# Delta rule of a three-layer trunk: modulation loads of four row tiles, one transpose for a group, multiplies from GpSimd to VectorE, substitution beside the recurrence

## The chip, the core and the metric

The program runs on one core of one Trainium2 chip. The metric is the device time of one execution in microseconds (us). Three executions of the kernel before took 2703.0, 2703.69 and 2696.82 us; the median is 2703.0 us.

The core's engines are named as the profile names them: PE is TensorE's matmul stream and PEld its loads of weights, DVE is VectorE, ACT is ScalarE, POOL is GpSimd, SP is the queue that issues most of the loads. Each engine runs its own list of instructions in order; a scheduler at build time writes these lists from the program, with semaphores between engines.

## The reference

A hybrid block (window attention beside a gated delta rule, both gated and merged, then an MLP), followed by two more layers. All is fp32, 512 latent tokens and 256 context tokens of width 1024. The change lies in the delta rule of the first block and in what is run beside it. Cut to that:

```python
# 8 heads of 64, chunks of 64 tokens, two directions; 6 tiles of 128 tokens = 12 chunks a direction
kk     = einsum('bhnid,bhnjd->bhnij', kc, kc)
t_mat  = eye(64) + bc[..., :, None] * dec_strict * kk
w_mat  = triangular_solve(t_mat, (bc * eG)[..., None] * kc)      # unit lower triangular
u_v    = triangular_solve(t_mat, bc[..., None] * vc)
intra  = dec_incl * einsum('bhnid,bhnjd->bhnij', qc, kc)
q_dec  = eG[..., None] * qc
k_tail = exp(g_last[..., None] - G)[..., None] * kc
def step(S, xs):                                                   # lax.scan over the 12 chunks
    u = uv_c - w_c @ S
    o = qd_c @ S + intra_c @ u
    S = exp(gl_c) * S + k_tail_c.T @ u
    return S, o
# beside it, independent of it: modulations silu(c) @ w_ada + b_ada of both conditioning vectors,
# and the attention half of the merge: sigmoid(gate_a) * (y_a @ w_br_attn)
```

## The kernel before

The work around the change is `delta`, a method that block 1 calls after its projections. It treats six token tiles (order 0, 1, 2, 5, 3, 4), in three groups of two steps of both directions; a group holds 64 triangular systems of 64 (chunk, step, direction, head). Its parts are Python generators:

- `prep(t)` makes a tile's matrices: `M` (decay times k k^T times the write strength b), and for latent tiles `R` (the masked intra-chunk matrix) and `qd` (q times its decay). The multiplies by b (L936), by the mask (L944) and of qd (L946) are on POOL.
- `subst(g)` inverts the 32 x 32 diagonal blocks of a group by substitution. Four DVE transposes of 32 partitions each (L957) make `Lw` from `M`; then come 31 steps of a DVE multiply into `tmp` (L964) and a DVE subtract into `X` (L966).
- `merges(g)` makes the inverses of the 64 x 64 systems from `X`: eight DVE transposes of 32 partitions (L981, L982) into two arrays `O1` and `O2`, products of 32 x 32 (L990, L1000, L1003) with a copy `Pm` on ACT between them (L994), and copies into place on ACT (L1006) and DVE (L1007).
- `chain(g, d)` is the recurrence of one direction over a group's two tiles. It loads k and v and scales them on POOL (L1021), makes `WT` (L1034, copied on ACT at L1036) and the first part of `u` (L1043). Per chunk it adds WT times the state to `u` (L1055), copies `u` on ACT (L1057), scales the old state into `Sg` on POOL (L1061), multiplies k and u into `d` (L1068) and sets the new state S = Sg + d on DVE (L1077; L1075 for the first). Per latent tile it then makes the output: for each half of 64 partitions four products of qd and S (L1084), then eight of R and u (L1087).
- `output` norms, gates and transposes the finished tiles of the last group (L1104 to L1121), after which the first dense product of the merge can start (L449 on `yDh`).

Two generators of other work run beside the recurrence. `attn_half` makes the attention half of the merge (PE products L449 on `yAh` and `yAl`, the split of the weights into `whi` on ACT and `wlo` on POOL at L731, the gate's multiply on DVE at L740). `ada` makes modulations: a load of one row tile (128 rows) by 512 columns, 256 KB, on the SP queue (L194), then one fp32 matmul of 32 output columns by 512 (L203) into one of four 32-partition groups of a PSUM bank; there are 96 such loads. `behind` holds each step of this other work behind the last but one product of the recurrence.

The order of the parts comes from `weave` and `side_by_side`, which take steps of several generators in proportion to given numbers of steps, and from the scheduler. Before: all preps with `subst(0)` between them, beside dense products; then `merges(0)`, `subst(1)` and `subst(2)` beside the rest of the dense products; then the recurrence of groups 0, 1 and 2 with `merges(1)` beside group 0 and `merges(2)` beside group 1:

```python
self.weave((seq(merges(0, *N, op), subst(1), subst(2)), 72), (early[0], early[1] - 20))
...
self.weave((seq(self.side_by_side((both(0), 28), (mg[1], 8)), self.side_by_side((both(1), 28), (mg[2], 8)),
                both(2)), 105), *[(self.behind(x, marks), n) for x, n in late(ch)])
```

## Time and profile before

| what | value |
|---|---|
| median of three executions | 2703.0 us |
| span of the profiled execution, first to last instruction | 2700.1 us |
| PE busy | 2514.3 us, 93% |
| PEld busy | 2108.0 us, 78% |
| DVE busy | 1498.9 us, 56% |
| ACT busy | 976.2 us, 36% |
| POOL busy | 992.4 us, 37% |
| mean granted TensorE clock | 0.961 |

The profile was taken on one execution; its time as a run is not given beside its span, so the span is what sums are made against, and the median lies 2.9 us above it. Busy shares are means over stages with different limits. The stage of the change lies between about 398 us and 712 us of the span: at 398 us DVE is in `subst(0)` and the preps, at 469 us `merges(0)` starts, at 512 us the first state is set, at 696 us the last `u` is done, and at 711.7 us the first dense product on the recurrence's result starts.

### The profile page before, as it was taken

What the parts mean: (1) busy time and instruction counts of PE and PEld (TensorE: products, weight loads), DVE (VectorE), ACT (ScalarE), POOL (GpSimd) and SP (SyncE); (2) the same over time, 40 slices, a digit from 0 to 9 for tenths busy, and PEclk for the clock granted to TensorE, in tenths of its full rate; (3) what the DMA queues carried; (4) which work ended last, traced back from release to release, by engine and by line L of the source; (5) the groups of instructions that cost most, each with busy time, mean ns of one, the idle gap of its engine ahead of it and who ended that gap; (6) DMA issues with size and microseconds to landing.
All of it is one profiled execution on the core that took longest, in us unless ns stands there. A gap on an engine that the chain in (4) does not pass through costs nothing.

```text
span 2700.1 us, 39906 instructions
## 1 busy us (share of the span) xinstructions
PE 2514.3 (93%) x15890; PEld 2108.0 (78%) x15890; DVE 1498.9 (56%) x2449; ACT 976.2 (36%) x1788; POOL 992.4 (37%) x829
## 2 busy tenths in 40 slices
PE   5897997799889999999999999999999999999998
PEld 3786875456677778889887888888888887888888
DVE  4556559993458972252585695757225447522225
ACT  3545443122342322342474522222223356423332
POOL 2443214534453323355334522333234623523331
PEclk8998998799899999999999999999999999999999
DMA  7231264455724643221012153434212101322231
GB/s 257 73 96 47 77 163 146 133 182 161 242 82 158 186 154 99 95 73 48 9 37 93 59 156 113 153 98 145 63 63 63 62 13 47 102 94 94 94 107 50
DMA packets 237625, 282.53 MB, mean 105 GB/s; under 512 B 12935, under 2 KB 183550, under 8 KB 237182
## 3 DMA queue, kind: packets, MB, share of 16 engines
q1 hardware_dynamic: 214062, 249.87, 29.6%
q10 hardware_dynamic: 23376, 30.11, 3.4%
q8 instruction: 125, 2.05, 0.3%
q14 instruction: 62, 0.51, 0.1%
HBM read 264.06 MB, written 15.88 MB: 104 GB/s over the span
## 4 chain that ended last, share of the span: by engine, by line
PE 72%; DVE 16%; DMA 4%; issue 4%; ACT 3%; POOL 1%; SPq 0%; ACTq 0%; POOLq 0%; DVEq 0%
PE mm L449 58%; DVE aacc L244 3%; DMA wada<-in_w_ada_dram 3%; PE mm L203 2%; PE sc L1796 2%; PE mm L1821 1%; DVE nt L315 1%; DVE wlo L108 1%; DVE X L966 1%; DVE tmp L964 1%; PE u L1055 1%; PE mm L1830 1%; PE mm L1327 1%; DMA wst<-in_w_in_dram 1%; PE mm L1084 1%
## 5 line engine op out<-in xcount | busy, mean ns | idle before, releaser
L108 POOL TENSOR_TENSOR wlo<-wst,whi 128x1024 fp32r<-128x1024 f32 (+2 forms) x143 | 374.3, 2619 | 812.4 <-ACT whi L437 798.5
L437 ACT ACTIVATE whi<-wst 128x1024 fp32r<-128x1024 f32 (+2 forms) x293 | 288.1, 1031 | 662.1 <-PE mm L449 365.6
L449 PE MATMUL mm<-hmxl,whi 128*128 128x512 f32 (+1 forms) x816 | 314.6, 387 | 5.0 <-DVE hmxl L318 2.7
L449 PE MATMUL mm<-hmxh,whi 128*128 128x512 f32 (+1 forms) x816 | 310.7, 386 | 7.3 <-ACT hmxh L317 7.3
L449 PE MATMUL mm<-hmxh,wlo 128*128 128x512 f32 (+1 forms) x816 | 312.6, 385 | 2.8 <-DVE wlo L108 2.8
L449 PE MATMUL mm<-hidxl,whi 128*128 128x512 f32 (+1 forms) x720 | 280.7, 390 | 7.7 <-DVE hidxl L1451 7.5
L449 PE MATMUL mm<-hidxh,wlo 128*128 128x512 f32 (+1 forms) x720 | 280.1, 389 | 1.1 <-DVE wlo L108 1.1
L108 DVE TENSOR_TENSOR wlo<-wst,whi 128x1024 fp32r<-128x1024 f32 (+1 forms) x150 | 184.4, 1232 | 170.8 <-ACT whi L437 170.7
L449 PE MATMUL mm<-hidxh,whi 128*128 128x512 f32 (+1 forms) x720 | 277.3, 388 | 0.0
L244 DVE SCALAR_TENSOR_TENSOR aacc<-wada,silu,aacc 128x512 f32<-128x512 f32 x280 | 244.7, 922 | 27.4 <-DMA wada<-in_w_ada_dram 27.0
L331 DVE SCALAR_TENSOR_TENSOR xres<-mm,mod,xres 128x512 f32<-128x512 f32 (+1 forms) x122 | 85.1, 703 | 236.0 <-PE mm L449 235.8
L1447 POOL TENSOR_TENSOR nsq<-nt 128x512 f32<-128x512 f32 (+1 forms) x134 | 135.5, 1014 | 151.6 <-ACT nt L1446 128.7
L449 PEld LDWEIGHTS mm<-hmxl,whi 128*128 128x128 f32 x816 | 158.2, 194 | 36.2 <-DVE hmxl L318 4.0
L449 PEld LDWEIGHTS mm<-hmxh,whi 128*128 128x128 f32 x816 | 156.6, 194 | 37.9 <-ACT hmxh L317 8.3
L449 PEld LDWEIGHTS mm<-hmxh,wlo 128*128 128x128 f32 x816 | 157.9, 194 | 33.8 <-DVE wlo L108 4.0
L1451 DVE TENSOR_TENSOR hidxl<-nsq,hidxh 128x512 fp32r<-128x512 f32 (+1 forms) x102 | 74.7, 732 | 168.2 <-POOL nsq L1447 165.7
L449 PEld LDWEIGHTS mm<-hidxl,whi 128*128 128x128 f32 x720 | 136.1, 189 | 38.3 <-DVE hidxl L1451 10.5
L449 PEld LDWEIGHTS mm<-hidxh,wlo 128*128 128x128 f32 x720 | 136.2, 189 | 30.2 <-DVE wlo L108 2.0
L449 PEld LDWEIGHTS mm<-hidxh,whi 128*128 128x128 f32 x720 | 136.2, 189 | 28.1
L1446 ACT ACTIVATE nt<-mm 128x512 f32<-128x512 f32 (+1 forms) x134 | 69.6, 521 | 231.6 <-PE mm L449 228.7
L449 PE MATMUL mm<-hh,whi 128*128 128x512 f32 x256 | 106.0, 414 | 7.5 <-DVE cy L625 3.3
L449 PE MATMUL mm<-whi,h2xh 128*128 128x256 f32 x384 | 110.1, 289 | 3.0 <-ACT raw L1579 2.6
(521 smaller groups left out, 6204.0 us busy)
## 6 DMA issues: line engine op xcount, KB each, us to landing
wst<-in_w_mlp_dram SPq DMA_DIRECT2D x96, 1024.0 KB, 5.4
wada<-in_w_ada_dram SPq DMA_DIRECT2D x256, 256.0 KB, 3.0
wst<-in_w_in_dram SPq DMA_DIRECT2D x35, 1024.0 KB, 5.5
wst<-in_w_out_dram SPq DMA_DIRECT2D x10, 1024.0 KB, 7.4
wada<-in_w_ada_dram SPq DMA_DIRECT2D x8, 1024.0 KB, 14.3
xacc<-in_w_out_dram SPq DMA_DIRECT2D x16, 256.0 KB, 2.9
Gb<-grows SPq DMA_DIRECT2D x12, 256.0 KB, 4.9
kc<-tok_k ACTq DMA_DIRECT2D x12, 256.0 KB, 3.6
```

The costliest lines, as they stand in the source:

```text
L108: e.tensor_tensor(out, x, hi.bitcast(F32), ALU.subtract)
L203: nc.tensor.matmul(ps[32 * g:32 * g + 32, :], sT[:, k, 30 - 2 * i:62 - 2 * i], loaded[x][:, k - k0, :], start=i == 0 and k < 4, stop=i == ...
L244: nc.vector.scalar_tensor_tensor(acc[j], wt, c, acc[j], ALU.mult, ALU.add)
L315: nc.vector.scalar_tensor_tensor(t, x[:, k, :], a(k), self.rb[n], ALU.mult, ALU.mult)
L331: nc.vector.scalar_tensor_tensor(x[:, m, :], ps[:, :T], gate(m, n), x[:, m, :], ALU.mult, ALU.add)
L437: self.nc.scalar.activation(hi[:, :, c0:c1], st[:, :, c0:c1], AF.Copy)
L449: self.nc.tensor.matmul(ps, lhs[a](k), rhs[b](k), start=first and i == 0, stop=last and i == n - 1)
L964: nc.vector.tensor_tensor(t, Lw[:, j + 1:, j:j + 1].to_broadcast([P, n, w]), x[:, j:j + 1, 0:w].to_broadcast([P, n, w]), ALU.mult)
L1446: nc.scalar.activation(t, ps[:, :T], AF.Relu)
L1447: nc.gpsimd.tensor_tensor(s2, t, t, ALU.mult)
L1451: self.latest = nc.vector.tensor_tensor(lo, s2, hi.bitcast(F32), ALU.subtract)
L1796: mm = nc.tensor.matmul(ps[:, c0:c1], QT_[:, w, t * P:(t + 1) * P], KT_[:, c0:c1], start=w == 0, stop=w == 1)
```

## The change

It leaves the arithmetic of the result as it is and alters how and where it is done:

1. `ada` loads four row tiles by 256 columns (512 KB) instead of one row tile by 512 (256 KB): 48 loads instead of 96, each followed by four matmuls of 32 x 256 into the four partition groups, one behind the other.
2. `subst`: ACT copies the four diagonal blocks of `M` into the other X buffer, and one DVE transpose of 128 partitions makes `Lw`.
3. `merges`: two DVE transposes of 128 partitions, into `Z2` and `Z1`, instead of eight of 32; the products read `Z1` and `Z2`, and eight ACT copies place their blocks into `O`. There is one `O` for a group (instead of two), in `M[0]` and `M[1]` for the later groups.
4. Multiplies go from POOL to DVE: M by b, R by the mask, qd (now straight from the PSUM tile of the transposes), the scaling of k and v, Sg, `wlo` of `attn_half`, and the gate z of `output`.
5. The output of a latent tile makes the R products first, alternating between the two halves of the partitions, then those of qd and S.
6. `merges(0)` alone stands beside the rest of the dense products; `subst(1)` and `merges(1)` run beside the recurrence of group 0, `subst(2)` and `merges(2)` beside that of group 1. The given numbers of steps are 160 (105 before) and 50 for the modulations (25 before).

Comments and docstrings go too, so line numbers shift by a few: L203 becomes L201, L449 L447, L957 L960 (with the ACT copies at L959), L964 and L966 become L967 and L969, L981 and L982 L984 and L985 (with the ACT copies at L1011), L994 L997, L1021 L1029, L1061 L1069, L1077 L1085, L1084 L1096, L1087 L1092.

```diff
-    def ada(self, pool, sT, w, bias, mod, n0, n1, kc=4, depth=1, bufs=None):
+    def ada(self, pool, sT, w, bias, mod, n0, n1, W=512, depth=1, bufs=None):
...
-        parts = [(i, k) for i in range(nb) for k in range(0, KT, kc)]
+        parts = [(i, k, c) for i in range(nb) for k in range(0, KT, 4) for c in range(0, 512, W)]
...
-                nc.tensor.matmul(ps[32 * g:32 * g + 32, :], sT[:, k, 30 - 2 * i:62 - 2 * i], loaded[x][:, k - k0, :],
-                                 start=i == 0 and k < 4, stop=i == nb - 1 and k >= 4)
+            for g in range(4):
+                nc.tensor.matmul(ps[32 * g:32 * g + 32, c:c + W], sT[:, k0 + g, 30 - 2 * i:62 - 2 * i],
+                                 loaded[x][:, g, :], start=i == 0 and k0 == 0 and c == 0,
+                                 stop=i == nb - 1 and k0 > 0 and c + W == 512)
...
-                        nc.gpsimd.tensor_tensor(lo, st, hi.bitcast(F32), ALU.subtract)
+                        nc.vector.tensor_tensor(lo, st, hi.bitcast(F32), ALU.subtract)
...
+                if src is qt:
+                    qd4 = qd.rearrange("p (d r) t -> p d r t", d=2)
+                    nc.vector.tensor_tensor(qd4, qd4, pt.rearrange("p (r t) -> p r t", t=P).unsqueeze(1)
+                                            .to_broadcast([P, 2, 4, P]), ALU.mult)
...
-                nc.gpsimd.tensor_tensor(m, m, b, ALU.mult)
+                nc.vector.tensor_tensor(m, m, b, ALU.mult)
...
+            Md = self.T(one, [P, 32, 32], f"X{1 - g % 2}")
             for b in range(4):
                 sl, cs = slice(32 * b, 32 * b + 32), slice(32 * (b % 2), 32 * (b % 2) + 32)
-                nc.vector.transpose(Lw[sl], M[g][sl, :, cs].rearrange("a p r -> a r p"))
+                nc.scalar.activation(Md[sl], M[g][sl, :, cs], AF.Copy)
+            nc.vector.transpose(Lw, Md.rearrange("a p r -> a r p"))
...
-            for b in range(4):
-                sl, cs = slice(32 * b, 32 * b + 32), (lo, hi)[b % 2]
-                nc.vector.transpose(O1[sl, :, cs].rearrange("a p r -> a r p"), x[sl])
-                nc.vector.transpose(O2[sl, :, cs].rearrange("a p c -> a c p"), x[sl].rearrange("a r c -> a c r"))
-                yield
+            Z1, Z2 = (self.T(pool, [P, 32, 32], n, bufs=1) for n in ("Z1", "Z2"))
+            nc.vector.transpose(Z2.rearrange("a p c -> a c p"), x.rearrange("a r c -> a c r"))
+            nc.vector.transpose(Z1.rearrange("a p r -> a r p"), x)
+            yield
...
+                if q0 == 0:
+                    for b in range(4):
+                        sl, cs = slice(32 * b, 32 * b + 32), (lo, hi)[b % 2]
+                        for d, z in enumerate((Z1, Z2)):
+                            nc.scalar.activation(parts(O[sl], d)[:, :, :, cs], parts(z[sl], d), AF.Copy)
...
-                    nc.gpsimd.tensor_tensor(x, y, dl[f][:, t, d, :].unsqueeze(2).to_broadcast([P, 8, CH]), ALU.mult)
+                    nc.vector.tensor_tensor(x, y, dl[f][:, t, d, :].unsqueeze(2).to_broadcast([P, 8, CH]), ALU.mult)
...
-                            nc.gpsimd.tensor_tensor(
+                            nc.vector.tensor_tensor(
                                 Sg[e], S0[e, :, e], dl["egs"][e, c, d, t, :].unsqueeze(2).to_broadcast([CH, 4, CH]),
                                 ALU.mult)
...
+                    for h in range(8):
+                        for c in half:
+                            nc.tensor.matmul(ps[c, h * CH:(h + 1) * CH], R[c, d, h, :], u[c, h, :],
+                                             start=h == 0, stop=False)
                     for c, S0 in states:
                         for r in range(4):
                             nc.tensor.matmul(ps[half[c], r * P:(r + 1) * P], qd[:, d, r, half[c]], S0[:, r, :],
-                                             start=r == 0, stop=False)
-                        for h in range(8):
-                            nc.tensor.matmul(ps[half[c], h * CH:(h + 1) * CH], R[half[c], d, h, :], u[half[c], h, :],
-                                             start=False, stop=h == 7)
+                                             start=False, stop=r == 3)
...
-        self.weave((seq(merges(0, *N, op), subst(1), subst(2)), 72), (early[0], early[1] - 20))
+        O = [self.T(op, [P, 32, CH], "O0"), M[0], M[1]]
+        self.weave((merges(0, O[0], op), 5), (early[0], early[1] - 20))
...
-        self.weave((seq(self.side_by_side((both(0), 28), (mg[1], 8)), self.side_by_side((both(1), 28), (mg[2], 8)),
-                        both(2)), 105), *[(self.behind(x, marks), n) for x, n in late(ch)])
+        nxt = lambda g: (seq(subst(g), merges(g, O[g], op)), 37)
+        self.weave((seq(self.side_by_side((both(0), 28), nxt(1)), self.side_by_side((both(1), 28), nxt(2)),
+                        both(2)), 160), *[(self.behind(x, marks), n) for x, n in late(ch)])
```

On PE, in the recurrence of group 1, the kernel before has these rows: modulation products (L203, out of a `wada` tile) stand singly or in twos and fours between products of the recurrence.

```order
L1055 MATMUL u_6117<-S_715_4527,WT_946_6042 64x128 x4
L203 MATMUL mm_953_6090<-wada_6180,silu_90_410 32x512
L203 MATMUL mm_953_6090<-wada_6183,silu_90_410 32x512
L1084 MATMUL mm_987_6261<-S_715_4527,qd_3919 64x128 x2
L203 MATMUL mm_953_6090<-wada_6186,silu_90_410 32x512
L1084 MATMUL mm_987_6261<-S_715_4527,qd_3919 64x128 x2
L1087 MATMUL mm_988_6290<-u_970_6144,R_3999 64x64
L203 MATMUL mm_953_6090<-wada_6227,silu_90_410 32x512
```

After, at the same kind of place (the start of group 1, beside the products of its `merges`), the modulation products (L201) come in fours, half as wide, from one `wada` tile.

```order
L201 MATMUL mm_725_4440<-wada_4995,silu_93_423 32x256 x4
L993 MATMUL mm_829_5166<-Z_821_5044,M_595_3399 32x32 x32
L201 MATMUL mm_725_4440<-wada_5022,silu_93_423 32x256 x4
L201 MATMUL mm_725_4440<-wada_5092,silu_93_423 32x256 x4
L1051 MATMUL u_5334<-vc_789_4834,M_594_3398 64x64
L1051 MATMUL u_5370<-vc_795_4868,M_594_3398 64x64
L201 MATMUL mm_725_4440<-wada_5160,silu_93_423 32x256 x4
```

The four of one load have moved together. On ACT, where `merges(0)` makes the first group's inverses, the kernel before goes from the loads and the weight split straight to the copies `Pm`.

```order
L1018 DMA kc_753_4671<-tok_k_448 128x512
L1019 DMA vc_754_4672<-tok_v_449 128x512
L994 ACTIVATE Pm_4134<-mm_687_4101 32x512 x2
L1006 ACTIVATE O_685_4079<-mm_689_4137 32x8x32
L994 ACTIVATE Pm_4207<-mm_690_4174 32x512 x2
```

After, the eight copies into `O` (L1011) and the four of the next group's diagonal blocks (L959, `X` out of `M`) stand ahead of the first `Pm` (L997).

```order
L1026 DMA kc_751_4552<-tok_k_448 128x512
L1027 DMA vc_752_4553<-tok_v_449 128x512
L1011 ACTIVATE O_686_4081<-Z_688_4095 32x2x8x32 x4
L1011 ACTIVATE O_686_4081<-Z_687_4094 32x2x8x32 x4
L959 ACTIVATE X_718_4403<-M_595_3399 32x1024 x4
L997 ACTIVATE Pm_4167<-mm_694_4134 32x512 x2
```

Twelve copies have come ahead of what the second product of `merges(0)` reads. On DVE, at the end of `subst(1)`, the kernel before has the last step, four transposes for the next group, eight for this one, and then the next group's steps.

```order
L966 TENSOR_TENSOR X_699_4268<-X_699_4268,tmp_4269 128x31
L957 STREAM_TRANSPOSE Lw_4382<-M_596_3400 32x1024 x4
L981 STREAM_TRANSPOSE O_712_4524<-X_699_4268 32x32x32
L982 STREAM_TRANSPOSE M_594_3398<-X_699_4268 32x32x32
...
L964 TENSOR_TENSOR tmp_4384<-Lw_4382,X_704_4383 128x31
L740 TENSOR_TENSOR ga_4773<-mm_803_4965,ga_4773 128x512
L1077 TENSOR_TENSOR S_715_4527<-Sg_813_5017,d_5071 64x4x64 x2
```

After, two transposes stand there, and behind them states (L1085), scalings of k (L1029) and of states (L1069), which POOL had before.

```order
L969 TENSOR_TENSOR X_716_4401<-X_716_4401,tmp_4402 128x31
L729 TENSOR_TENSOR wlo_4650<-wst_4645,whi_4649 128x512
L738 TENSOR_TENSOR ga_4534<-mm_768_4674,ga_4534 128x512
L984 STREAM_TRANSPOSE Z_821_5044<-X_716_4401 128x32x32
L985 STREAM_TRANSPOSE Z_820_5043<-X_716_4401 128x32x32
L1085 TENSOR_TENSOR S_709_4388<-Sg_766_4661,d_4699 64x4x64 x2
L1085 TENSOR_TENSOR S_712_4391<-Sg_769_4688,d_4718 64x4x64 x2
L1029 TENSOR_TENSOR kb_790_4835<-kc_788_4833,gnb_947 128x512
L1069 TENSOR_TENSOR Sg_803_4909<-S_709_4388,gegs_895 64x256 x2
L1069 TENSOR_TENSOR Sg_805_4927<-S_712_4391,gegs_895 64x256 x2
```

Nine transposes fewer stand around that place (the one into `Lw` comes nine rows further on), and the multiplies of the recurrence have come into DVE's list. From the end of `delta` on, the engines' lists are the same in both kernels but for a few exchanged neighbours.

## Rows read from the trace of the kernel before

**Rows 1.** Windows (start:end length, busy us and instructions by engine, clock, DMA share, GB/s):

```profile
core 0: us, PE busy (x) PEld busy (x) DVE busy (x) ACT busy (x) POOL busy (x), PEclk, DMA share, GB/s
398.00:469.00 71.00, 51.95 (x445) 40.90 (x443) 66.60 (x103) 23.60 (x31) 32.12 (x20) 0.89 0.49 149
469.00:512.00 43.00, 27.14 (x462) 17.19 (x462) 41.26 (x59) 7.61 (x16) 25.85 (x34) 0.62 0.36 115
512.00:696.00 184.00, 177.06 (x2254) 109.27 (x2254) 111.76 (x177) 41.79 (x82) 65.46 (x75) 0.97 0.57 179
696.00:712.00 16.00, 8.55 (x54) 5.22 (x54) 8.38 (x16) 3.54 (x7) 3.24 (x2) 0.71 0.54 191
```

**Rows 2.** Chain that ended last, 469 to 712: first piece, first PE piece of eight (start, us):

```profile
468.13 1.93 DVE O L981
...
518.34 3.64 PE mm L449 x8
```

**Rows 3.** Window of L203 alone (PE and PEld busy), 512 to 696:

```profile
512.00:696.00 184.00, 57.78 (x162) 8.06 (x162) 0.97 0.57 179
```

**Rows 4.** PE timeline, modulation products (start, us, two or eight records):

```profile
522.52 1.05 PE L203 MATMUL mm<-wada,silu 128*32 128x512 f32 x2
...
618.40 1.06 PE L203 MATMUL mm<-wada,silu 128*32 128x512 f32 x8
```

**Rows 5.** Window of L1087 alone (PE and PEld busy), 512 to 696:

```profile
512.00:696.00 184.00, 17.52 (x234) 15.10 (x234) 0.97 0.57 179
```

**Rows 6.** PE timeline, products of 64 x 64, halves not alternating and alternating:

```profile
653.34 1.09 PE L1087 MATMUL mm<-u,R 64*64 64x64 f32 x16
...
669.79 1.14 PE L1043 MATMUL u<-vc,O 64*64 64x64 f32 x31
```

**Rows 7.** Timeline of POOL and DVE around 420 us:

```profile
419.82 2.47 POOL L944 TENSOR_TENSOR R<-R,gmask 128x1024 f32<-128x1024 f32 x1
420.05 2.40 DVE L966 TENSOR_TENSOR X<-X,tmp 128x135 f32<-128x135 f32 x1
...
423.19 0.34 DVE L964 TENSOR_TENSOR tmp<-Lw,X 128x175 f32<-128x175 f32 x1
```

**Rows 8.** DVE groups, 398 to 468, substitution (busy us, mean ns, idle before):

```profile
L966 DVE TENSOR_TENSOR X<-X,tmp 128x31 f32<-128x31 f32 (+15 forms) x31 | 22.2, 717 | 0.9
L964 DVE TENSOR_TENSOR tmp<-Lw,X 128x31 f32<-128x31 f32 (+15 forms) x31 | 15.8, 508 | 0.9
```

**Rows 9.** DVE groups, 398 to 712, other lines:

```profile
L957 DVE STREAM_TRANSPOSE Lw<-M 32x1024 f32<-32x1024 f32 x12 | 23.6, 1964 | 2.2 <-POOL M L936 2.1
L1077 DVE TENSOR_TENSOR S<-Sg,d 64x256 f32<-64x256 f32 x40 | 16.7, 418 | 44.7 <-PE d L1068 43.1 <-POOL Sg L1061 0.8
L981 DVE STREAM_TRANSPOSE O<-X 32x1024 f32<-32x1024 f32 x8 | 15.5, 1933 | 0.6 <-POOL M L936 0.5
...
L740 DVE TENSOR_TENSOR ga<-mm,ga 128x512 f32<-128x512 f32 x8 | 5.5, 690 | 3.2 <-issue 3.0
...
L906 DVE TENSOR_TENSOR Gb<-Gb,gG 128x1024 f32<-128x1024 f32 x4 | 4.9, 1220 | 3.2 <-DMA Gb<-grows 3.2
```

**Rows 10.** ACT groups, 371 to 712:

```profile
L917 ACT ACTIVATE Gb<-Gb 128x1024 f32<-128x1024 f32 x6 | 6.3, 1056 | 22.5 <-DVE Gb L906 22.5
```

**Rows 11.** Line L247, a DVE transpose of 128 partitions (lowest, median, highest ns):

```profile
L247 DVE STREAM_TRANSPOSE wada<-aacc x40: 662/711/715, 840.8 to 1892.7; 128x512 f32<-128x512 f32 x40
```

**Rows 12.** Timeline of several engines: first Pm, first state, first dense product:

```profile
481.16 1.20 ACT L994 ACTIVATE Pm<-mm 32x512 f32<-32x512 f32 x2 [10.18 <-PE mm L990]
...
511.94 0.88 DVE L1075 COPY S<-d 64x256 f32<-64x256 f32 x2
...
711.70 0.79 PE L449 MATMUL mm<-yDh,whi 128*128 128x512 f32 x1 [3.31 <-ACT whi L437]
```

**Rows 13.** Page, DMA issues (KB each, us from issue to landing):

```profile
wada<-in_w_ada_dram SPq DMA_DIRECT2D x256, 256.0 KB, 3.0
wst<-in_w_in_dram SPq DMA_DIRECT2D x35, 1024.0 KB, 5.5
```

55 lines of the change are left out of this document (23 added, 32 removed).

## The prediction

> **What bounds the kernel now.** I read the windows first, to cut the stage into stretches by which engine is full [rows 1]. From 398 to 469 us DVE is busy 66.6 of 71 us, with the steps of `subst(0)` and the preps, while PE is busy 52. From 469 to 512 DVE is busy 41.3 of 43 us and PE 27.1, at a granted clock of 0.62. From 512 to 696 it turns: PE is busy 177.1 of 184 us at 0.97, DVE 111.8. The last 16 us are a tail of short dependent steps. Then I read the chain that ended last, and look where it changes engine: it starts the second stretch with L981, the first of a row of transposes on DVE, and has its first PE piece of eight matmuls at 518 [rows 2]. So a saving on DVE counts before 512 us and a saving on PE after it. The instants that bound the stretches are the first `Pm` at 481.2, the first state at 511.9 and the first dense product at 711.7 [rows 12]. Outside the stage the lists of both kernels are the same, so only it can move the time.
>
> **First stretch, 398 to 469: +3 us.** DVE is the bound, so I add and remove on DVE. A multiply of 128 x 512 costs 0.69 us there (L740), one of 128 x 1024 costs 1.22 (L906) [rows 9]. Coming in are ten multiplies of M by b (6.9), four of R by the mask and four of qd (8 x 1.22 = 9.8) and, by the order, nine scalings of k and v (6.2): 22.9 us. Going out are four transposes into `Lw` at 1.96, of which one, now of 128 partitions, stays: -5.9. Whether a 128-partition transpose costs more than one of 32 partitions no row shows for this shape; L247 turns 128 x 512 in 0.71 us [rows 11], so partitions seem to cost nothing by themselves, and I take 1.95, the price of L957 and L981 (bounds: 0.7, and four times 1.95).
>
> The other thing that goes is a stretching of DVE's steps. A subtract of 128 x 135 took 2.40 us while POOL's multiply by the mask ran 2.47 us beside it; a multiply of more elements, 128 x 175, took 0.34 us with POOL quiet [rows 7], and 176 is the mean number of elements over the 31 steps (31 to 256). The 62 instructions of `subst(0)` take 22.2 + 15.8 = 38.0 us in this stretch [rows 8]; at 0.34 each they would take 21. So 17 us of stretching go with the POOL multiplies (bounds 0 and 17). The Trainium skill ("SBUF — State Buffer", section "SBUF: two separate sides") says that a VectorE instruction with two SBUF inputs contends with a GpSimd instruction only if that one reads SBUF; the memsets left on GpSimd read nothing, so by it all 17 go. No row here shows a memset beside a subtract; if those stretched too, some of the 17 would stay.
>
> A new wait is for ACT: four copies of a diagonal block ahead of the one transpose. A copy of as many elements in a partition takes 1.06 [rows 10]; 4.2 us, of which I count 3 as not covered by other DVE work. The sum: 22.9 - 5.9 - 17 + 3 = +3.
>
> **Second stretch, 469 to 512: -3 us.** On DVE eight transposes (8 x 1.93 = 15) become two (3.9), and the four into the next `Lw` behind them become one. But `Pm` waits on ACT, which now has eight copies into O (half of 1.06 each by their size: 4.2) and the four diagonal copies (4.2) ahead of it [rows 10]: 469 + 3 + 3.9 + 8.4 and a hop is about 485, against 481.2 now [rows 12]. What is behind `Pm` (the second products, the first WT and u) comes those 4 us later, and gets them back because DVE has neither the `Lw` transposes nor finished substitution steps ahead of the merge's own copies. I take 512 again for the first state, 3 us less than the first stretch has added; the bounds are 505 and 518.
>
> **Third stretch, 512 to 696: -38 us.** PE is the bound. The modulation products are 57.8 of its 177.1 us [rows 3]. A run of two records, which is one matmul, takes 1.05 us; a run of eight, four matmuls in four groups of columns, takes 1.06 [rows 4]. So four run together, and a lone one costs as much as four. The change always sends four, half as wide: 0.53 us a load (half of 1.06, an estimate). Of the 48 loads an eighth falls before 512, as now; 42 x 0.53 = 22.3, which takes off 35.5 us. Bounds: 0.50 and 0.75 a load, the last if the loads of the stationary operands show: 21 and 32 us.
>
> The R products take 17.5 us [rows 5]. Sixteen records that stay in one half take 1.09 us, 68 ns each; 31 that alternate between the halves take 1.14, 37 ns each [rows 6]. At 37 ns the 234 records take 8.7 us: -8.8, or 0 if alternating gives nothing here.
>
> PE's work is then 177.1 - 35.5 - 8.8 = 132.8 us. How full PE will be is the choice that matters; it is 96% full now. DVE gets 40 multiplies Sg at 0.42 (by L1077, the same shape), 27 scalings at 0.69 and twelve multiplies for `wlo` and z (8.3): 44 us. It loses 15 transposes (29) [rows 9] and stretching. From 111.8 it goes to 127 at most, and I take 117, with a third of the 38 us that the substitutions have here gone as stretching as in the first stretch it was nearly half. That is 80% of what is left instead of 61%, and the list is in order: an add that makes a state can stand behind a substitution step or a scaling of 0.3 to 0.7 us, and each direction has twelve chunks. So I take 5 points off the filling: 91%, 146 us. The SP queue has the same bytes in half as many loads; its DMA share of 0.57 [rows 1] times 184/146 is 0.72, and loads of 1 MB with the same rows of 256 columns land in 5.5 us, those of 256 KB in 3.0 [rows 13], so three loads ahead cover one load each 3 us.
>
> **Tail: 0.** One multiply of a tile goes from POOL to DVE, in front of nothing.
>
> **Sum.** 3 - 3 - 38 = -38. The span goes from 2700.1 to 2662 us, and the median, 2.9 above it, from 2703.0 to 2665.
>
> **The rivals.**
>
> Poorer filling: PE waits for DVE. For it speaks that states, scalings and two substitutions share one list, and that group 1 can't begin before `subst(1)` and `merges(1)` are through; against it that DVE has 29 us to spare. At 80% the 132.8 us take 166: -18, about 2685 (2676 to 2697).
>
> The other side, the clock. It is 0.62 in the stretch where PE is busy 63% of the time, 0.89 at 73%, 0.97 at 96% [rows 1]; eight L449 records took 3.64 us shortly after the low stretch [rows 2]. The change takes 44 us of work from PE and puts waits between its bursts, so the clock could fall in the third stretch. With a mean granted clock c and 13 us of waits it lasts 132.8 / c + 13; that is 184, no gain, at c = 0.78. At 0.70 it lasts 203: +19, 2722 (2711 to 2750). Against it: at a filling near 90% the neighbouring rows are 0.89 and 0.97, a cost of 5 us or so. The Trainium skill ("TensorE: Matmul & The Clock Gate", section "Why this matters for your kernels") has the rule that idle gaps between bursts of matmuls bring the clock down; the clocks of these windows agree with it.
>
> More than forecast: the second stretch shrinks too. DVE loses 11 us of serial transposes there; if the twelve ACT copies slip in beside PE, the first state comes 11 us sooner. With 95% filling the third stretch is 140: 3 - 11 - 44 = -52, about 2651 to 2633. Against it: `Pm` stands behind the copies in ACT's list.
>
> The transposes don't do what the change says: one of 128 partitions costs four of 32. Then DVE has 146 us in the third stretch and 6 more in the first, and becomes the bound: about 2700. L247 speaks against it [rows 11].
>
> **How the numbers follow.** Forecast, 2650 to 2676: 0.60. Poorer filling: 0.17. More: 0.12. Clock: 0.07. Transposes: 0.04. The range is 2640 to 2694: it takes in nearly all of the poorer filling and half of the greater gain, and leaves out the clock, the transposes and the ends, about 2 in 10. The forecast's own range comes from the filling (86 to 96%: 154 to 138 us) and the bounds of a modulation load. A measurement of this kernel tells about 0.3%, 8 us, from no change. Faster by more: forecast, greater gain and most of the poorer filling, 0.88. Within it: the ends of the poorer filling and the transposes, 0.05. Slower: the clock, 0.07.
>
> **What would show it.** Modulation products in runs of eight records of about 0.53 us, 25 us in all; R products at 37 ns a record; transposes of 128 partitions near 1.95 us; substitution instructions at a mean near 0.34; the first `Pm` near 485 and the first state near 512; PE busy about 133 us from there to the last `u` near 658, at a clock above 0.9; the first dense product near 674. The prediction is wrong if PE waits 30 us or more for DVE in that stretch, if its clock is under 0.8, or if modulation loads come late.

## The result and the profile after

The changed kernel took 2671.85 us (median of four executions, 2670.01 to 2681.77) against 2703.35 us of the kernel before in the same comparison. The medians differ by 31.5 us. The ratio of the executions is 0.9899 with a 95% interval of 0.9879 to 0.9919, which is 27 us (22 to 33). The forecast was 2665 us in a range of 2640 to 2694. The profiled execution has a span of 2669.4 us, 30.7 less than before.

The windows of the changed kernel, cut at the first state and at the end of the last `u`:

```profile
core 0: us, PE busy (x) PEld busy (x) DVE busy (x) ACT busy (x) POOL busy (x), PEclk, DMA share, GB/s
398.00:469.00 71.00, 53.91 (x459) 42.24 (x457) 60.26 (x121) 28.91 (x37) 8.25 (x16) 0.87 0.55 171
469.00:511.00 42.00, 23.09 (x475) 17.50 (x472) 31.74 (x72) 15.72 (x27) 2.16 (x4) 0.62 0.28 88
511.00:659.90 148.90, 141.22 (x2401) 104.02 (x2401) 103.87 (x227) 55.80 (x102) 4.32 (x4) 0.93 0.66 212
```

Against [rows 1], the first two stretches together are 1 us shorter than before, and the third has shrunk from 184 to 149 us: PE is busy 141 us instead of 177, at a clock of 0.93 instead of 0.97. POOL is nearly empty. The timeline of several engines, for the instants of [rows 12]:

```profile
473.81 1.90 DVE L984 STREAM_TRANSPOSE Z<-X 128x1024 f32<-128x1024 f32 x1
475.80 5.10 ACT L1011 ACTIVATE O<-Z 32x512 f32<-32x512 f32 x8 [6.79 <-DVE Z L984]
480.91 4.25 ACT L959 ACTIVATE X<-M 32x1024 f32<-32x1024 f32 x4
485.18 1.20 ACT L997 ACTIVATE Pm<-mm 32x512 f32<-32x512 f32 x2
...
510.98 0.87 DVE L1083 COPY S<-d 64x256 f32<-64x256 f32 x2
...
658.81 1.04 PE L1063 MATMUL u<-S,WT 128*64 128x128 f32 x8
...
675.53 0.80 PE L447 MATMUL mm<-yDh,whi 128*128 128x512 f32 x1 [2.42 <-ACT whi L435]
```

The copies into O and of the diagonal blocks stand ahead of `Pm`, as the order had shown; `Pm` comes at 485.2, the first state at 511.0, the last `u` ends at 659.9 and the first dense product starts at 675.5, 36.2 us sooner than before. Then the modulation products alone, as a window and as pieces of PE's timeline ([rows 3, 4] before):

```profile
511.00:659.90 148.90, 28.29 (x328) 7.54 (x328) 0.93 0.66 212
```

```profile
515.68 0.64 PE L201 MATMUL mm<-wada,silu 128*32 128x256 f32 x8
519.73 1.07 PE L201 MATMUL mm<-wada,silu 128*32 128x256 f32 x16
```

A load's group of four (eight records) takes 0.64 us by itself and about 0.53 where two follow each other; the 41 groups of this window have a mean of 0.69. The R products, with the records that [rows 5] is for, are in the windows from the first state to the last `u` and to 674 us, and the piece of the timeline shows them at 36 ns each ([rows 6]):

```profile
511.00:659.90 148.90, 9.52 (x224) 7.98 (x224) 0.93 0.66 212
511.00:674.00 163.00, 10.67 (x256) 8.99 (x256) 0.92 0.67 219
```

```profile
661.81 1.15 PE L1092 MATMUL mm<-u,R 64*64 64x64 f32 x32
```

And the groups of DVE from 398 to 674 us, for [rows 8, 9]:

```profile
L967 DVE TENSOR_TENSOR tmp<-Lw,X 128x31 f32<-128x31 f32 (+15 forms) x93 | 31.8, 342 | 2.5
L969 DVE TENSOR_TENSOR X<-X,tmp 128x31 f32<-128x31 f32 (+15 forms) x93 | 31.8, 342 | 2.3
L1085 DVE TENSOR_TENSOR S<-Sg,d 64x256 f32<-64x256 f32 x40 | 16.7, 418 | 12.7 <-PE d L1076 12.2
L1029 DVE TENSOR_TENSOR vc<-vc,gbe 128x512 f32<-128x512 f32 x12 | 8.2, 685 | 8.0 <-DMA vc<-tok_v 8.0
L960 DVE STREAM_TRANSPOSE Lw<-X 128x1024 f32<-128x1024 f32 x3 | 6.1, 2027 | 10.3 <-ACT X L959 10.3
L984 DVE STREAM_TRANSPOSE Z<-X 128x1024 f32<-128x1024 f32 x3 | 5.9, 1957 | 0.0
L985 DVE STREAM_TRANSPOSE Z<-X 128x1024 f32<-128x1024 f32 x3 | 5.8, 1945 | 0.0
L904 DVE TENSOR_TENSOR Gb<-Gb,gG 128x1024 f32<-128x1024 f32 x4 | 4.9, 1225 | 13.1 <-DMA Gb<-grows 13.1
```

The steps of the substitution have a mean of 342 ns, the transposes of 128 partitions take what one of 32 took. With only memsets and four small instructions (8 elements in a partition) left on POOL, nothing of the stretching is left in these means. By the Trainium skill ("SBUF — State Buffer", section "SBUF: two separate sides"), a VectorE instruction with two SBUF inputs contends only with a GpSimd instruction that reads SBUF; the means agree with it.

### The profile page after: what moved, and what is told of

Read it like the earlier page. It is cut to its first block, busy times and chain, and to the rows that moved or that the text cites. A ratio compares the mean times of both kernels' runs of the same rounds, so it can differ in the third digit from the quotient of the medians.

```text
span 2669.4 us, 40169 instructions
## 1 busy us (share of the span) xinstructions
PE 2477.8 (93%) x16082; PEld 2106.8 (79%) x16082; DVE 1481.0 (55%) x2530; ACT 1005.0 (38%) x1824; POOL 878.4 (33%) x721
## 4 chain that ended last, share of the span: by engine, by line
PE 69%; DVE 15%; DMA 7%; issue 4%; ACT 3%; POOL 1%; SPq 0%; ACTq 0%; POOLq 0%; DVEq 0%
PE mm L447 59%; DMA wada<-in_w_ada_dram 4%; DVE aacc L242 3%; PE sc L1804 2%; DVE nt L313 1%; PE mm L1829 1%; DVE wlo L108 1%; DMA Gb<-grows 1%; PE mm L1838 1%; PE mm L1335 1%; PE u L1063 1%; DVE tmp L967 1%; DVE X L969 1%; PE mm L201 0%; ACT whi L435 0%
## 5 line engine op out<-in xcount | busy, mean ns | idle before, releaser
L447 PE MATMUL mm<-hmxl,whi 128*128 128x512 f32 (+1 forms) x816 | 315.2, 388 | 5.6 <-DVE hmxl L316 3.5
L447 PE MATMUL mm<-hmxh,whi 128*128 128x512 f32 (+1 forms) x816 | 311.5, 386 | 6.4 <-ACT hmxh L315 6.4
L447 PE MATMUL mm<-hmxh,wlo 128*128 128x512 f32 (+1 forms) x816 | 313.5, 386 | 2.5 <-DVE wlo L108 2.5
L447 PE MATMUL mm<-hidxl,whi 128*128 128x512 f32 (+1 forms) x720 | 280.9, 390 | 9.6 <-DVE hidxl L1459 9.6
L447 PE MATMUL mm<-hidxh,wlo 128*128 128x512 f32 (+1 forms) x720 | 280.0, 389 | 1.6 <-DVE wlo L108 1.6
L447 PE MATMUL mm<-hidxh,whi 128*128 128x512 f32 (+1 forms) x720 | 277.4, 388 | 0.0
L447 PEld LDWEIGHTS mm<-hmxl,whi 128*128 128x128 f32 x816 | 158.5, 194 | 36.8 <-DVE hmxl L316 4.7
L447 PEld LDWEIGHTS mm<-hmxh,whi 128*128 128x128 f32 x816 | 157.4, 195 | 36.8 <-ACT hmxh L315 7.3
L447 PEld LDWEIGHTS mm<-hmxh,wlo 128*128 128x128 f32 x816 | 158.6, 195 | 33.7 <-DVE wlo L108 3.8
L447 PEld LDWEIGHTS mm<-hidxl,whi 128*128 128x128 f32 x720 | 136.3, 189 | 40.0 <-DVE hidxl L1459 12.2
L447 PEld LDWEIGHTS mm<-hidxh,wlo 128*128 128x128 f32 x720 | 136.3, 189 | 30.8 <-DVE wlo L108 2.5
L447 PEld LDWEIGHTS mm<-hidxh,whi 128*128 128x128 f32 x720 | 136.2, 189 | 28.2
L447 PE MATMUL mm<-whi,h2xh 128*128 128x256 f32 x384 | 109.6, 288 | 4.5 <-ACT raw L1587 2.6
L447 PE MATMUL mm<-hh,whi 128*128 128x512 f32 x256 | 105.7, 413 | 7.1 <-DVE cy L623 3.3
```

Source lines behind the costliest of these rows:

```text
L447: self.nc.tensor.matmul(ps, lhs[a](k), rhs[b](k), start=first and i == 0, stop=last and i == n - 1)
```

## The experiments

The theory behind the forecast, called A, is that PE's work is the bound behind the first state and the modulation products are its main term. The first rival, B, is that the order (substitutions beside the recurrence) and the transposes bring the gain. What the runs forced instead is called D below. Each run is given by its ratio to the kernel before on the same chip, and by the time at which its first dense product starts in its profile (711.7 before, 675.5 changed), since the stretch behind that instant varies between profiles by itself. The kernels before in the comparisons had medians of 2699.0 us (the modulation loads alone, the loads taken back, the old order, the multiplies on POOL), 2698.2 us (the old order of R, the narrow transposes, the full-width loads, `Pm` first) and 2702.0 us (the other four), so a time is read beside its own. The changed kernel, at 0.9899, would be at 2671.8, 2670.9 and 2674.7 us beside these. The price of a part is the difference of two ratios times the median.

### One part alone, and parts taken back

**The modulation loads alone, on the kernel before.**

```diff
-            ada = self.ada(pool, sT, w_ada, v["b_ada"], self.mod, 4, 12, 1, 3, 4)
+            ada = self.ada(pool, sT, w_ada, v["b_ada"], self.mod, 4, 12, 256, 1, 2)
```

(with `ada` of the changed kernel and its number of steps, 50, and two buffers with one load ahead instead of four with three).

> The kernel before with the modulation loads and products of the change alone (four row tiles by 256 columns, two buffers and one load ahead, since the memory holds no more there). Theory A, after the first state PE's work is the bound and the modulation products are the main term: their 58 us there become about 30, so 2674 to 2684 us. Theory B, the order brings the gain (substitution beside the recurrence, fewer transposes) and modulation products only fill what would stand idle: 2695 us or more. If the single load ahead comes too late, PE waits for wada in the trace.

Measured: ratio 1.0009 (0.9995 to 1.0023), 2700.52 us; the first dense product at 707.8. The window from the first state to the last `u`:

```profile
508.50:695.30 186.80, 165.26 (x2450) 119.56 (x2451) 116.50 (x179) 41.39 (x82) 65.90 (x75) 0.84 0.60 186
```

Theory A is wrong in this form, and the time lies in B's range. The products are shorter, but the stretch isn't: PE waits, and its clock is 0.84 instead of 0.97, so that what is left takes longer. PE is idle for 21.5 us of it, 14.6 more than before. Its busy time at 0.84 would be 143 us at 0.97 (165.3 x 0.84 / 0.97, an estimate), so the clock takes 22 us, more than the waits. The list of PE's waits in that stretch (us in total, times, longest) begins:

```profile
PE mm L201 <- DMA wada<-in_w_ada_dram: 7.6, 6, 2.9
PE mm L447 <- DVE ga L738: 7.1, 3, 5.0
PE u L1053 <- DVE S L1073: 4.5, 1, 4.5
PE mm L988 <- DVE M L980: 3.4, 2, 3.0
```

Most of it is for DVE. The 7.6 us for `wada` belong to the shallow prefetch, one load ahead. That it alone is to blame is ruled out by the run with the narrow transposes below, which has three loads ahead and no gain either.

**The modulation loads taken back, in the changed kernel.**

```diff
-            ada = self.ada(pool, sT, w_ada, v["b_ada"], self.mod, 4, 12, 256, 3, 4)
+            ada = self.ada(pool, sT, w_ada, v["b_ada"], self.mod, 4, 12, 1, 3, 4)
```

(with `ada` of the kernel before and its number of steps, 25).

> The changed kernel with the old modulation loads (one row tile by 512 columns, lone matmuls of 32 x 512). Theory A: about 28 us of PE work come back in the third stretch, 2694 to 2704 us. Theory B: 2680 us or less.

Measured: 0.9995 (0.9983 to 1.0007), 2699.54 us, first dense product at 704.3. The same window:

```profile
510.00:692.00 182.00, 177.28 (x2249) 103.79 (x2249) 104.37 (x228) 55.36 (x101) 4.32 (x4) 0.98 0.58 178
```

Here A holds and B fails: with the old products PE is 97% busy again, and all the rest of the change is worth nothing by the ratio (its first dense product starts 7 us sooner than before). So the products are needed, and by the run before they don't suffice.

**The old order of the parts.**

```diff
-        self.weave((merges(0, O[0], op), 5), (early[0], early[1] - 20))
+        self.weave((seq(merges(0, O[0], op), subst(1), subst(2)), 69), (early[0], early[1] - 20))
...
-        nxt = lambda g: (seq(subst(g), merges(g, O[g], op)), 37)
+        nxt = lambda g: (merges(g, O[g], op), 5)
```

(and 105 steps instead of 160).

> The changed kernel with the substitutions of groups 1 and 2 ahead of the recurrence again, beside merges(0) and the dense rest, and the old numbers of steps (the diagonal blocks of group 2 go through the buffer of Z1). Theory A: DVE has 42 us of substitution steps there and the first state moves from 511 to 515 or 520, but the PE work behind it is the same: 2676 to 2684 us. Theory B: 2690 us or more.

Measured: 0.9918 (0.9904 to 0.9933), 2678.64 us, first dense product at 687.1. That is in A's range for the time, but not by A's way: the first state came earlier, at 506.9 us, and the third stretch was longer, 166.5 us against 148.9, with PE at a clock of 0.86:

```profile
506.90:673.40 166.50, 145.33 (x2408) 106.38 (x2412) 109.13 (x237) 51.54 (x97) 4.32 (x4) 0.86 0.61 191
```

**The multiplies back on POOL**, all that the change had moved:

```diff
-                nc.vector.tensor_tensor(m, m, b, ALU.mult)
+                nc.gpsimd.tensor_tensor(m, m, b, ALU.mult)
...
-                    nc.vector.tensor_tensor(x, y, dl[f][:, t, d, :].unsqueeze(2).to_broadcast([P, 8, CH]), ALU.mult)
+                    nc.gpsimd.tensor_tensor(x, y, dl[f][:, t, d, :].unsqueeze(2).to_broadcast([P, 8, CH]), ALU.mult)
```

(and so R by the mask, qd, Sg, `wlo` and z).

> The changed kernel with all the moved multiplies back on POOL. Theory A: the steps of the substitutions are stretched again by 17 us in the first stretch, but 23 us of multiplies leave DVE there, so about 0; behind the first state PE is the bound, 0 to 8 us more: 2668 to 2680 us. Theory B: the stretching and POOL's slower Sg in each chunk cost the recurrence 15 us or more: 2688 us or more.

Measured: 0.9887 (0.9871 to 0.9904), 2668.67 us, first dense product at 672.4. The moved multiplies bring nothing, although the steps of the substitution are stretched again, by the groups of DVE from 390 to 674 us:

```profile
L969 DVE TENSOR_TENSOR X<-X,tmp 128x31 f32<-128x31 f32 (+15 forms) x93 | 51.1, 549 | 2.9
L967 DVE TENSOR_TENSOR tmp<-Lw,X 128x31 f32<-128x31 f32 (+15 forms) x93 | 46.9, 504 | 2.9
```

98 us instead of 64, and yet the first transpose into Z starts at 465.2 us, 8.6 sooner than in the changed kernel. The window up to there:

```profile
398.00:465.20 67.20, 51.80 (x451) 41.23 (x449) 60.12 (x99) 27.95 (x36) 32.91 (x23) 0.90 0.50 152
```

DVE is busy 60.1 us and idle 7.1; in the changed kernel it is busy 62.6 and idle 13.2 up to its Z. So stretching and the multiplies themselves weigh nearly alike on DVE there, as in the sum of the first stretch, and most of the 8.6 us are waits. Behind the first state they don't weigh alike: DVE is busy 81.0 us there instead of 103.9, but the stretch is 150.6 us long, no shorter.

**The old order of the R products** (per half of the partitions, qd and then R):

```diff
-                    for h in range(8):
-                        for c in half:
-                            nc.tensor.matmul(ps[c, h * CH:(h + 1) * CH], R[c, d, h, :], u[c, h, :],
...
+                        for h in range(8):
+                            nc.tensor.matmul(ps[half[c], h * CH:(h + 1) * CH], R[half[c], d, h, :], u[half[c], h, :],
```

> The changed kernel with the R and qd products in the old order (per half of the partitions, qd then R). Theory A, PE bounds the stretch behind the first state also after the change: R goes from 37 back to 68 ns a record, 8 us more PE work, 2677 to 2682 us. Theory C, with the emptier PE such work hides in waits: 2674 us or less.

Measured: 0.9962 (0.9946 to 0.9979), 2688.55 us, first dense product at 685.1. PE's window between the first state and the last `u`, and R's group there:

```profile
509.10:672.80 163.70, 154.75 (x2435) 116.24 (x2434) 104.49 (x228) 55.75 (x102) 4.28 (x4) 0.91 0.60 192
```

```profile
L1095 PE MATMUL mm<-u,R 64*64 64x64 f32 x240 | 18.3, 227 | 0.0
```

R is back at 18 us for 240 records, about 8 more than in the changed kernel, and the stretch is longer by 15. PE's work counts here, so C fails, but the time is 6.5 us above A's range too. Where the rest comes from isn't shown: the ratio makes the price 17 us, the first dense product 9.6, and the profile of this run has the longest part behind that instant of all (1997.5 us).

**The narrow transposes** instead of the wide ones:

```diff
-                nc.scalar.activation(Md[sl], M[g][sl, :, cs], AF.Copy)
-            nc.vector.transpose(Lw, Md.rearrange("a p r -> a r p"))
+                nc.vector.transpose(Lw[sl], M[g][sl, :, cs].rearrange("a p r -> a r p"))
...
-            nc.vector.transpose(Z2.rearrange("a p c -> a c p"), x.rearrange("a r c -> a c r"))
-            nc.vector.transpose(Z1.rearrange("a p r -> a r p"), x)
+            for b in range(4):
+                sl = slice(32 * b, 32 * b + 32)
+                nc.vector.transpose(Z2[sl].rearrange("a p c -> a c p"), x[sl].rearrange("a r c -> a c r"))
+                nc.vector.transpose(Z1[sl].rearrange("a p r -> a r p"), x[sl])
```

> The changed kernel with the narrow transposes (four of 32 partitions into Lw, eight into Z1 and Z2, no copies of diagonal blocks on ACT); the copies from Z1 and Z2 into O stay. DVE gets 27 transposes of 1.95 us more, 53 us in all, 23 of them behind the first state, where it is now busy 105 of 149 us. Theory A, PE is the bound there and DVE has room: the first stretches pay some 5 to 8 us, the third little, 2676 to 2684 us. Theory D, PE and DVE both bound the third stretch once the modulation products are short: 2690 us or more, which would explain why those products alone gained nothing on the kernel before.

Measured: 1.0031 (1.0014 to 1.0049), 2708.87 us, first dense product at 711.3. Theory D's case:

```profile
522.50:696.30 173.80, 146.77 (x2407) 108.57 (x2407) 132.02 (x242) 51.29 (x97) 4.32 (x4) 0.87 0.57 180
```

```profile
PE mm L993 <- DVE Z L984: 11.0, 3, 6.0
PE u L1063 <- DVE S L1085: 5.0, 2, 4.4
```

(the second fence is the head of PE's list of waits there). DVE is busy 132 of 174 us, not full, but PE waits for its transposes and states: PE is idle for 27 us instead of 7.7, and its clock went to 0.87. Loads are asked for three ahead here, and `wada` isn't in its list. The first state comes at 522.5 us, 11.5 later than in the changed kernel, so the narrow transposes cost 11.5 us ahead of it and 25 behind it.

### Where PE's time goes when it is freed

**Twice the products, on the run with the modulation loads alone.** This separates "PE is still the bound" from "PE's freed time was lost".

```diff
-            for g in range(4):
+            for y, g in [(y, g) for y in range(1 + twice) for g in range(4)]:
...
-        nc.vector.tensor_copy(res, ps)
+        nc.vector.tensor_scalar(res, ps, 0.5 if twice else 1.0, None, ALU.mult)
```

> The kernel before with the new modulation loads, every group of four products done twice and the sum halved, so that PE has about 31 us more work in the stage and the result is the same. In the run with each group once the third stretch was 187 us long with PE at a mean clock of 0.84 and DVE's substitution steps and transposes in front of it. Theory D, DVE and the chain of the recurrence set that stretch and PE's freed time was lost to waits and a lower clock: the clock rises above 0.92 and the time stays within 8 us of that run, so 2693 to 2709 us. Theory A, PE is the bound all the same: 25 us or more longer, 2722 us or more.

Measured: 1.0037 (1.0021 to 1.0053), 2709.69 us, 0.7 us above D's range and 12 below A's; by the ratios it is 7.6 us above the run with each group once. Its window between the first state and the last `u`:

```profile
512.50:702.10 189.60, 173.18 (x2768) 122.17 (x2769) 113.88 (x178) 41.42 (x82) 65.69 (x75) 0.92 0.58 181
```

318 more records lengthen the stretch by 2.8 us, and the clock is 0.92 instead of 0.84. So PE's work wasn't the bound in the run with the loads alone, and a fuller PE ran at a higher clock. The first state is 3.9 us later than there, and 2.1 us more lie between the last `u` and the first dense product (716.6).

**Two parts alone: the modulation loads and the wide transposes**, that is, the changed kernel with the POOL multiplies, the order of R and the order of the parts as before. Its edits are those of the runs with the old order, the multiplies on POOL and the old order of R, together.

> Two parts of the change alone: the new modulation loads and the wide transposes (with one O for a group and its copies on ACT); the multiplies are on POOL, the R products in the old order and the substitutions ahead of the recurrence. Taken from the changed kernel one at a time, order, R and POOL moved the end of the stage by +12, +10 and -3 us. Theory D, the modulation products free PE and the transposes free DVE, and only both together shorten the stretch: about half of the gain stands, 2680 to 2692 us. Rival: the gain needs all parts, 2695 us or more.

Measured: 0.9920 (0.9906 to 0.9934), 2679.27 us, first dense product at 684.7. The point estimate of the two parts is 0.8% of the 1.0% that the change brings. Its third stretch:

```profile
502.60:672.30 169.70, 151.52 (x2442) 112.31 (x2444) 82.39 (x163) 52.17 (x98) 66.19 (x77) 0.90 0.60 190
```

The loads alone gave nothing, and the transposes with all the rest but the loads gave nothing; both together give most of the gain. The transposes alone on the kernel before weren't run, and against the run with the loads alone this one has three loads ahead too. The gain is also made up in another way than that of the changed kernel: the first state comes 9.3 us sooner than before, and the third stretch is only 14 us shorter, not 35. The other three parts add the remaining 0.2%, some 6 us, although taken from the whole change one at a time they move it by 17 (R), 5 (order) and -3 us (POOL), and by 9.6, 11.6 and -3.1 us at the first dense product: such prices don't add.

### Versions that might go further

**Full-width loads** of four row tiles by 512 columns:

```diff
-            ada = self.ada(pool, sT, w_ada, v["b_ada"], self.mod, 4, 12, 256, 3, 4)
+            ada = self.ada(pool, sT, w_ada, v["b_ada"], self.mod, 4, 12, 512, 1, 2)
```

> The changed kernel with modulation loads of four row tiles by all 512 columns (1 MB, 24 loads, two buffers of twice the size, one load ahead) and four matmuls of 32 x 512 behind each. A group of half width was seen to take 0.64 us in place of my 0.53, one of full width 1.06: 24 x 1.06 = 25 us against 48 x 0.64 = 31, so 5 us less PE work. Theory A: 2665 to 2669 us. Rival: one load ahead is too little, PE waits for wada and the time is 2673 us or more.

Measured: 0.9882 (0.9859 to 0.9905), 2665.92 us, in A's range but not to be told from the changed kernel; its first dense product starts at 678.0, no sooner. Its third stretch:

```profile
509.50:665.10 155.60, 143.49 (x2238) 102.84 (x2238) 104.44 (x227) 55.07 (x101) 4.32 (x4) 0.88 0.62 203
```

Less PE work, 7 us more stretch, and a clock of 0.88. By itself this is inconclusive on the time.

**Pm first** in ACT's list:

```diff
-                            nc.scalar.activation(parts(O[sl], d)[:, :, :, cs], parts(z[sl], d), AF.Copy)
+                            with self.tc.issue_after(self.pm.ins):
+                                nc.scalar.activation(parts(O[sl], d)[:, :, :, cs], parts(z[sl], d), AF.Copy)
```

(and the copies of the diagonal blocks likewise).

> The changed kernel with the copies Pm of the first half of each merge ahead of the copies into O and of the diagonal blocks in ACT's list. If the twelve copies ahead of Pm set the first state, Pm comes 8 to 9 us sooner and the first state 4 to 8 us: 2664 to 2668 us. Rival: behind Pm the first products of the recurrence wait for the same copies into O, so nothing moves: 2670 to 2674 us.

Measured: 0.9940 (0.9923 to 0.9957), 2682.75 us: 11 us worse than the changed kernel. The first `Pm` came 4.0 us behind the first transpose into Z (474.3 and 470.3) instead of 11.4, but the first state 35.8 us behind it (506.1) instead of 37.2: for the first state the rival holds, what stands behind `Pm` waits for the same copies into O. The time is in neither range: the third stretch took 166.4 us at a clock of 0.88. Its list of waits has at the top:

```profile
PE mm L447 <- DVE ga L738: 8.0, 2, 4.3
PE mm L996 <- DVE M L1021: 4.8, 1, 4.8
```

Products of the attention half (L447) stand in PE's list ahead of work of the recurrence, and by this list they wait for DVE's multiply of the gate (L738). The scheduler's lists changed behind the edit, so this run tells that an edit which does nothing where it is made can cost 17 us behind it, not which instruction does it.

**Only the scalings of k and v on POOL**, the multiplies that wait for loads in DVE's list:

```diff
-                    nc.vector.tensor_tensor(x, y, dl[f][:, t, d, :].unsqueeze(2).to_broadcast([P, 8, CH]), ALU.mult)
+                    nc.gpsimd.tensor_tensor(x, y, dl[f][:, t, d, :].unsqueeze(2).to_broadcast([P, 8, CH]), ALU.mult)
```

> The changed kernel with only the scalings of k and v back on POOL. If these scalings, which wait for their loads in DVE's list ahead of the transposes into Z, are what holds the first stretch: Z comes at 466 to 469 in place of 474 us and the time is 2663 to 2669 us. Rival: the steps of the substitution are stretched by as much as is saved, 2670 to 2675 us.

Measured: 0.9907 (0.9891 to 0.9923), 2675.19 us, no change; Z at 476.2. The steps of the first substitution there, from 398 to 477 us:

```profile
L967 DVE TENSOR_TENSOR tmp<-Lw,X 128x31 f32<-128x31 f32 (+15 forms) x31 | 15.2, 491 | 0.7
L969 DVE TENSOR_TENSOR X<-X,tmp 128x31 f32<-128x31 f32 (+15 forms) x31 | 14.5, 466 | 0.6
```

The rival holds: these 62 steps take 29.7 us instead of 21.2, 8.5 more, and what left DVE's list ahead of Z is nine scalings of 0.69 us and a wait of 2.4 for a load, 8.6 us. Why Z is later still, by 2.4 us, isn't traced.

**All multiplies on POOL, with full-width loads**, the edits of two runs above together:

> The changed kernel with the multiplies back on POOL and modulation loads of all 512 columns (1 MB, two buffers). If both small effects seen alone add (DVE freed of scalings that wait for loads, 5 us less PE work): 2660 to 2665 us. If PE's work saved is given back as waits at a lower clock, as in the run of the wide loads alone (the third stretch was 156 us there against 149): 2666 to 2674 us.

Measured: 0.9859 (0.9839 to 0.9878), 2661.36 us, first dense product at 669.9. It is below the changed kernel (its interval ends where that of the changed kernel begins, 0.9878 and 0.9879) and some 11 us faster by the ratios. That is where the first forecast has it, that the two small effects add; from either of its two halves alone (0.9887 and 0.9882) the noise doesn't separate it:

```profile
509.70:657.80 148.10, 138.71 (x2243) 99.59 (x2241) 80.45 (x150) 55.18 (x100) 65.56 (x76) 0.93 0.62 204
```

DVE is down to 80 us there, and the clock is back at 0.93 with less PE work than in the changed kernel. It has the lowest ratio of all that ran.

## Why the prediction was right, and where a term was off

**What bounds the kernel.** The cut into stretches held: of the 36.2 us at the first dense product, 35 lie behind the first state and 1 before it. That the old modulation products in the changed kernel bring the time back, with PE 97% busy, shows that with them PE bounds the third stretch. What the prediction lacked was how close the next bound lies already in the kernel before: by its sum the shorter products are 35 of the 38 us, and alone they brought nothing. It had the poorer filling as a rival, with DVE in front of it, and the clock as another; the run with the loads alone shows both together on the kernel before (filled less, clock 0.84). The wide transposes are what kept the changed kernel from that. The prediction had them as a gain ahead of the first state, where the run with the narrow ones makes them worth 11.5 us, and as 29 us less on DVE in the third stretch; its last rival has them as a condition, with DVE as the bound and about 2700 us without them. The run with the narrow ones is near that case (2708.9 us) and shows the condition: 25 us in the third stretch, 36 in all by the ratio. DVE wasn't full there, as the rival has it, but PE waited for it and ran at a lower clock.

**First stretch, +3 us: it was +5.7** (Z at 473.8 instead of 468.1). The prices on DVE were sound: a mean of 342 ns for the steps (0.34 forecast), 0.69 and 1.22 us for the multiplies, transposes near 1.95. The windows up to Z, of the kernel before and of the changed kernel:

```profile
398.00:468.13 70.13, 51.95 (x445) 40.90 (x443) 65.73 (x102) 23.60 (x31) 31.25 (x20) 0.90 0.48 146
398.00:473.80 75.80, 55.10 (x467) 42.43 (x465) 62.61 (x127) 28.93 (x37) 8.25 (x16) 0.85 0.58 184
```

DVE's busy time fell by 3.1 us, where the forecast had its terms at 0. What came on top are waits: DVE is idle for 13.2 us instead of 4.4, and the forecast had 3 us more. The two longest:

```profile
408.51 1.23 DVE L904 TENSOR_TENSOR Gb<-Gb,gG 128x1024 f32<-128x1024 f32 x1 [6.61 <-DMA Gb<-grows]
473.20 0.69 DVE L1029 TENSOR_TENSOR vc<-vc,gbe 128x512 f32<-128x512 f32 x1 [2.38 <-DMA vc<-tok_v]
```

The first is for a load of decays (`Gb`). The four copies on ACT, for which the prediction booked its 3 us, were through at 406.2 us, inside this wait. In all 9.0 us of waits for `Gb` fall into the stretch, where the kernel before has none; why these loads come too late isn't shown. For the second, the chain that ended last of the changed kernel reads:

```profile
458.35 9.64 DMA wada<-in_w_ada_dram
468.01 5.17 DMA vc<-tok_v
473.20 0.69 DVE vc L1029
473.90 1.83 DVE Z L984
```

By the chain, ACT's queue issues a load of v at 468.0, when a modulation load has landed; DVE's list has the scaling of that v ahead of the transposes, so Z starts when v is there, 2.4 us after the last step of the substitution. In the kernel before that scaling is not in DVE's list. The modulation loads, 512 KB each, are asked for before the recurrence can use them; whether holding them back would bring the 2.4 us wasn't tried.

**Second stretch, -3 us: -6.6.** First state at 511.0 (512 forecast) and `Pm` at 485.2 (485 forecast), by the copies on ACT as worked out. That `Pm` hit so closely is luck in part: Z started 1.8 us later than forecast and the twelve copies took 9.4 us, not 8.4, but only one transpose stood ahead of them, not two. The run with `Pm` first shows that the copies cost the first state little by standing ahead of it, 1.4 us; they have to be done all the same.

**Third stretch, -38 us: -34.6** (148.9 instead of 183.5 us between the first state and the end of the last `u`, where the prediction had 146). The length was right within 3 us, in part by luck, because the misses offset each other: PE was busy 8.4 us longer than forecast and waited 5.5 us less. By its terms:

- The modulation products took 28.3 us, not 22.3. The step that was off is "0.53 us a load (half of 1.06)": a group by itself takes 0.64 and only a pair 1.07, and the mean was 0.69. The bounds given, 0.50 and 0.75, hold it.
- R went from 17.5 to 9.5 us before the end of the last `u`, with 1.2 more behind it: -8.0, where -8.8 was forecast, and the run with the old order gives about 8 as its price in PE work.
- The filling was 95%, not 91%: PE was busy 141.2 us, not 132.8, at a clock of 0.93. Part of this busy time is the clock. Worked out as busy times clock, an estimate, 141.2 x 0.93 = 131 us of PE work at the full clock, against 176.5 x 0.97 = 171 before. At 0.97 that work would take 135 us, so the clock cost 6 us; the prediction named about 5 for it among the rivals and left it out of the sum. Its rival divides 132.8 us, a time at 0.97, by the clock and so counts 0.97 twice: no gain would be at 0.75, not 0.78.
- The 5 points off the filling came from a DVE at 80%. It was at 70%: busy 103.9 us, where the prediction took 117 (127 less a third of 38 is 114).

By the same estimate the runs line up: loads alone 165.3 x 0.84 = 139, narrow transposes 146.8 x 0.87 = 128, old R order 154.8 x 0.91 = 141, `Pm` first 143.2 x 0.88 = 126. The work is within some 5 us of what the sum of the prediction says each time; what differs is how much of the stretch is waiting, and the clock, which makes the work longer. The clock doesn't follow the waiting strictly: with 8% of the stretch idle it was 0.88 in the run with the full-width loads and 0.94 in the one with the multiplies on POOL. By the Trainium skill ("TensorE: Matmul & The Clock Gate", section "Why this matters for your kernels"), idle gaps between bursts of matmuls bring the clock down. These rows agree in direction: 0.97 and 0.98 with at most 4% idle, 0.84 to 0.90 with 11% or more.

**Tail, 0:** 15.6 us from the last `u` to the first dense product, 16.3 before.

**Outside the stage.** The lists are the same, but of the 36.2 us at 675.5 us only 30.7 are left at the end. Two places take most of it: about 3 us where products wait for the parts of their inputs around 1150 us, and 2.4 us at 1555 us. There the windows that start at the same product, first of the kernel before and then of the changed kernel, show the clock:

```profile
1586.00:1592.00 6.00, 6.00 (x26) 4.87 (x27) 5.96 (x11) 0.00 (x0) 0.62 (x1) 1.00 0.38 102
```

```profile
1553.00:1559.00 6.00, 5.52 (x18) 4.43 (x19) 5.97 (x11) 0.00 (x0) 0.61 (x1) 0.72 0.28 76
```

From the first dense product to the end the profiles of this study take 1987.5 to 1997.5 us, and all their edits lie ahead of it. So a loss of this size is within what profiles differ by. Of the difference between the 38 us forecast and the 30.7 of the profiled span, 5.5 lie here and 1.8 in the stage; that the change has no part in the 5.5 isn't shown.

**Not shown:** that the multiplies moved to DVE help. The prediction booked 17 us of stretching and 23 of multiplies against each other in the first stretch, and the run with all of them back on POOL agrees: nothing, or slightly better. What stays open is what R's old order costs beyond its 8 us of work, with 17 us by the ratio and 9.6 at the first dense product; why the two parts alone leave a third stretch of 170 us; and which entries of the lists make `Pm` first slower.

## What to carry to other kernels

When PE is 96% busy, work taken from it is a gain only as far as the next engine's list can follow; try the part alone and the whole without the part, because a part can be worth nothing alone, the rest without it nothing either, and both together the gain. Matmuls that use one group of columns should be sent so that the four groups stand side by side, and products of half the partitions so that they alternate. Before multiplies are moved away from an engine to spare another its contention, set the time they take there against the stretching they cause: here the two were equal ahead of the first state, and behind it the 23 us by which the move filled DVE cost no time either.

## What the runs showed of the hardware

Work taken from PE came back as waits and a lower clock, over a stretch in which PE was still busy most of the time: with the modulation loads alone, 88% by the profile's busy time (165.3 of 186.8 us) and a granted clock of 0.84. With 318 records more in the same stretch the clock was 0.92 and the stretch 2.8 us longer. A DVE transpose of 128 partitions by 1024 took 1.95 us and one of 32 partitions by 1024 1.93, so a narrow one costs what a wide one does. Four fp32 products of 32 x 256 in the four groups of columns took 0.64 us by themselves and 1.07 where two such groups followed each other. Products of 64 x 64 that alternate between the halves of the partitions took 36 ns a record.
